# Memory projection and compression as float32 products, gates in one piece: a change to a two-layer decoder kernel

## The chip, the cores and the metric

The kernel runs on one core of one Trainium2 chip. The metric is the device time of one execution in microseconds (us); the median of several runs counts. Engines are named as the profile names them: PE is TensorE (PEld its weight loads), DVE is VectorE, ACT is ScalarE, POOL is GpSimd, SP is SyncE, which here only issues DMAs.

## What is computed

A decoder trunk of two layers on 512 tokens of width 1024, all in float32. Layer 0 is the one that the change touches. Its attention runs in three branches whose results are mixed by gates, beside a cross-attention to 256 memory tokens:

```python
mem_kv = rmsnorm(mem, mem_norm[layer]) @ w_mem_kv[layer]          # 256 x 1024 @ 1024 x 512
q, kc, vc, ks, vs, kw, vw, q_mem, gl = jnp.split(h @ a_w_in[i], A_SPLITS, axis=-1)

def compress(t, i):                                               # 31 blocks of 32 tokens, 3 heads
    tb = (t[:, :, blk_tok] + cmp_pos[i]).reshape(B, G, n_cmp, CMP_BLOCK * D)
    return jax.nn.gelu(tb @ cmp_w1[i] + cmp_b1[i]) @ cmp_w2[i] + cmp_b2[i]

gates = jax.nn.sigmoid(gate_logits)                               # 512 x 12 heads x 3 branches
return g_b[..., 0:1] * o_c + g_b[..., 1:2] * o_s + g_b[..., 2:3] * o_w
```

After attention come an output projection and a squared-ReLU MLP; layer 1 has dilated attention, the same memory attention with its own projection, and another MLP.

## The kernel before

**Products.** Nearly every large product is made of three products of type fp32r: an operand is split into a part rounded to fp32r and a residue, and `mm3` (L250 to L255) adds up high x high, high x residue and residue x high in PSUM. The split costs ScalarE a copy and VectorE or GpSimd a subtraction: `wsplit` (L246, L248) for weights, `part` (L269, L270) for activations with a gain, `split` (L288, L291) for the rest. Weights are fetched in tiles of 512 KB into a ring of three staging tiles `st` by SP's queue (`wload`, L234), and the split writes them to a ring of four working tiles `w`. A few products are plain float32: the probabilities times values (`pair`, L696, with two products side by side in the two halves of the array) and the last product of the compressed branch (L967).

**Order of the work.** The program is written as generators. In layer 0 a list of attention items (scores, softmax, scaling, transposes, output) runs in the foreground, and a list of background work is stepped at fixed ratios between the items. Within a generator, each `yield` is a place at which something else may come between. A scheduler then orders the instructions of each engine. Engines and DMA queues take their instructions strictly in that order.

**Start of layer 0.** `proj_a(0, ...)` makes queries, keys and values of the first head group; woven with its second half is the projection to `w_a0`, 420 columns wide (compressed keys and values, and 36 gate logits). Its evacuation `evac0` (L743 to L750) runs once for each of four blocks of 128 rows: ScalarE scales all 420 columns into a tile (L744), and the last 36 go through minus and clip (L747), exponential (L748), plus one (L749) and reciprocal (L750) to the sigmoid gates in the tile `ab`.

**The stage that the change touches.** Two generators are woven. `compress` makes for keys and for values: transposes of the projection (L805), copies of it and of a shifted copy (L811, L812), then in four steps sums with the position term on GpSimd (L825), a split (L288, L291), and 16 products of 96 x 256 (each one `mm3`) with the weights `w_c1`; `finish` applies the GELU (L844 to L853), transposes (L858) and multiplies by the small `w_c2` (six matmuls of 64 columns). `mem_kv(0, ...)` splits the normalised memory (L269, L270, 256 columns each) and makes 8 x 2 products of 128 x 512 (each one `mm3`) with `w_mem`, then the key norm and the values. Together they are the first entry of the background work; the projections of the next head groups follow.

**Softmax of the branches.** `attn_a`'s `front` makes the scores (L1004, L1017), the maximum (L1008, L1020) and the exponentials with their sums (L216), a reciprocal of the two sums (L1028), a multiplication of it by the two gates (L1029, 128 x 2), and GpSimd scales both probability tiles by that column (`pscale`, L684: two multiplications, the second by 1.0). `back` transposes the tiles (L1047, L1053).

## Time and profile before

| what | us |
|---|---|
| median of 3 runs | 1303.48 |
| lowest and highest of them | 1299.24 and 1312.04 |
| the profiled execution, its own time | 1296.79 |
| its span, from first to last instruction | 1295.0 |
| start of the 420-wide projection to the first product of the compression | 28.6 to 73.2 |
| compression and memory projection on TensorE | 73.2 to 107.2 |
| rest of the attention of layer 0 | 107.2 to 340 |

A row of the profile's views names the line, the engine, the operation and the tiles as output<-input, the shape, and how often; after the bar stand the busy time in us, the mean in ns, and the idle time just before, with what ended it. A row of a timeline begins with start and length in us. A row of windows begins with the stretch and its length, then gives by engine the busy time and the number of instructions (in the order PE, PEld, DVE, ACT, POOL), then the granted TensorE clock, the DMA share and GB/s; a window made for one line shows only the engines that run that line. A row of waits names who waited for whom, the total in us, how often, and the longest. A busy TensorE is not one at its peak, since the ends of its matmuls are modelled and overlap.

### The profile page before, as it was taken

How to read it: one execution, taken by the hardware profiler on the slowest of the kernel's cores; microseconds unless marked ns; L12 is line 12 of the kernel's file. 1: busy time of each engine (PE TensorE's matmuls, PEld its weight loads, DVE VectorE, ACT ScalarE, POOL GpSimd, SP SyncE). 2: the span in 40 equal slices, each digit the busy share in tenths (PEclk: the TensorE clock that was granted, in tenths of full speed). 3: DMA queues.
4: the chain of work that ended last, by engine and by line, in shares of the span. 5: the costliest groups of instructions: out<-in, count | busy, mean ns of one | idle time of the engine just before them, and what ended most of it. 6: DMA issues, size and time to landing. Idle time of an engine off the chain costs nothing.

```text
span 1295.0 us, 18552 instructions
## 1 busy us (share of the span) xinstructions
PE 1239.9 (96%) x6468; PEld 1026.0 (79%) x6468; DVE 858.9 (66%) x1597; ACT 770.5 (59%) x1699; POOL 380.9 (29%) x478
## 2 busy tenths in 40 slices
PE   9789998899999999999999989999999999999998
PEld 7668776678788888888887889887678888888887
DVE  6987767755565657566578567776667656656566
ACT  6775677774575364453657548777657445355462
POOL 4365684533140000000002779572424000000000
PEclk9899999999999999999999999999999999999999
DMA  7342322334478797897965331210249789698434
GB/s 262 116 128 89 98 98 90 66 75 115 139 248 232 239 267 221 261 234 222 284 202 176 104 112 50 69 45 9 85 151 291 217 271 245 211 282 231 141 111 162
DMA packets 61837, 215.28 MB, mean 166 GB/s; under 512 B 6736, under 2 KB 14928, under 8 KB 61232
## 3 DMA queue, kind: packets, MB, share of 16 engines
q1 hardware_dynamic: 50800, 143.72, 34.2%
q0 software_dynamic: 9344, 35.77, 14.0%
q10 hardware_dynamic: 1600, 34.61, 7.4%
q8 instruction: 51, 0.84, 0.3%
q14 instruction: 42, 0.34, 0.1%
HBM read 208.83 MB, written 72.35 MB: 217 GB/s over the span
## 4 chain that ended last, share of the span: by engine, by line
PE 67%; DVE 5%; ACT 4%; DMA 2%; POOL 2%; issue 2%; SPq 0%; POOLq 0%; ACTq 0%; DVEq 0%
PE s_ps L253 13%; PE s_ps L254 13%; PE s_ps L255 13%; PE s_acc L254 3%; PE s_acc L255 3%; PE s_acc L253 3%; PE s_pt L254 3%; PE s_pt L255 3%; PE s_pt L253 3%; PE s_po L696 2%; DVE s_w L248 1%; ACT s_p L216 1%; PE s_ps L1508 1%; ACT s_w L246 1%; DVE s_pt L216 1%
## 5 line engine op out<-in xcount | busy, mean ns | idle before, releaser
L248 DVE TENSOR_TENSOR s_w<-s_st,s_w 128x1024 fp32r<-128x1024 f32 (+3 forms) x240 | 287.1, 1200 | 256.7 <-ACT s_w L246 255.5
L246 ACT ACTIVATE s_w<-s_st 128x1024 fp32r<-128x1024 f32 (+4 forms) x272 | 263.8, 973 | 186.2 <-PE s_pt L255 44.0
L253 PE MATMUL s_ps<-s_act,s_w 128*128 128x512 f32 x568 | 221.7, 392 | 0.7 <-ACT s_act L288 0.7
L255 PE MATMUL s_ps<-s_act,s_w 128*128 128x512 f32 x568 | 221.8, 391 | 0.0
L254 PE MATMUL s_ps<-s_act,s_w 128*128 128x512 f32 x568 | 221.3, 390 | 0.0
L253 PEld LDWEIGHTS s_ps<-s_act,s_w 128*128 128x128 f32 x568 | 106.5, 188 | 23.8 <-ACT s_act L288 1.6
L255 PEld LDWEIGHTS s_ps<-s_act,s_w 128*128 128x128 f32 x568 | 106.6, 188 | 22.8 <-issue 0.8
L254 PEld LDWEIGHTS s_ps<-s_act,s_w 128*128 128x128 f32 x568 | 106.6, 188 | 21.9 <-DVE s_act L291 0.2
L216 ACT ACTIVATE s_p<-s_ps 128x512 f32<-128x512 f32 x64 | 38.2, 597 | 112.6 <-PE s_ps L255 112.6
L254 PE MATMUL s_acc<-s_w,s_act 128*128 128x512 f32 (+3 forms) x288 | 101.6, 354 | 3.1 <-POOL s_w L248 1.7
L253 PE MATMUL s_acc<-s_w,s_act 128*128 128x512 f32 (+3 forms) x288 | 101.3, 357 | 2.7 <-DVE s_tq L912 1.1
L1136 POOL DMA_DIRECT2D sum<-in_w_db_dram x16 | 14.4, 901 | 301.7 <-ACT s_p L216 300.0
L255 PE MATMUL s_acc<-s_w,s_act 128*128 128x512 f32 (+3 forms) x288 | 99.8, 351 | 0.0
L684 POOL TENSOR_SCALAR s_p<-s_p,s_cr 128x256 f32<-128x256 f32 (+3 forms) x128 | 73.5, 597 | 66.9 <-DVE s_cr L1029 14.5
L216 ACT ACTIVATE s_p<-s_ps,s_nm 128x256 f32<-128x256 f32 (+3 forms) x128 | 65.5, 522 | 16.3 <-DVE s_nm L1008 7.0
L248 POOL TENSOR_TENSOR s_w<-s_st,s_w 128x512 fp32r<-128x512 f32 (+4 forms) x32 | 55.4, 1732 | 50.0 <-ACT s_w L246 41.4
L253 PEld LDWEIGHTS s_acc<-s_w,s_act 128*128 128x128 f32 x288 | 54.5, 190 | 9.6 <-DVE s_tq L912 1.2
L254 PEld LDWEIGHTS s_acc<-s_w,s_act 128*128 128x128 f32 x288 | 54.7, 190 | 8.3 <-POOL s_w L248 2.3
L692 ACT ACTIVATE s_pt<-s_pt 128x512 f32<-128x512 f32 (+2 forms) x97 | 51.0, 529 | 15.5 <-PE s_pt L1053 5.4
L288 ACT ACTIVATE s_qk<-s_p 128x256 fp32r<-128x256 f32 (+1 forms) x96 | 46.9, 489 | 21.3 <-DVE s_p L1146 19.4
L255 PEld LDWEIGHTS s_acc<-s_w,s_act 128*128 128x128 f32 x288 | 54.6, 190 | 4.0
L1136 POOL DMA_DIRECT2D sum<-sum x16 | 14.1, 883 | 146.1 <-DMA sum<-sum 50.3
(334 smaller groups left out, 2959.2 us busy)
## 6 DMA issues: line engine op xcount, KB each, us to landing
s_st<-in_w_up_dram SPq DMA_DIRECT2D x64, 512.0 KB, 4.2
s_st<-sum SPq DMA_DIRECT2D x64, 512.0 KB, 6.8
s_st<-in_w_db_dram SPq DMA_DIRECT2D x48, 512.0 KB, 4.5
sum<-in_w_db_dram POOLq DMA_DIRECT2D x16, 1024.0 KB, 13.9
sum<-sum POOLq DMA_DIRECT2D x16, 1024.0 KB, 10.6
s_st<-in_w_bq_dram SPq DMA_DIRECT2D x16, 384.0 KB, 3.3
s_st<-in_w_ag_dram SPq DMA_DIRECT2D x11, 512.0 KB, 4.7
s_st<-in_w_c_dram SPq DMA_DIRECT2D x8, 512.0 KB, 3.6
```

What stands on the lines that cost most here:

```text
L216: return lambda *a, **k: self.marks.append(f(*a, **k))
L246: nc.scalar.activation(w[:, 0], st, AF.Copy)
L248: e.tensor_tensor(out=w[:, 1], in0=st, in1=w[:, 0], op=ALU.subtract)
L253: mm(ps, lh[0], rh[0], start=start, stop=False, skip_group_check=again)
L254: mm(ps, lh[0], rh[1], start=False, stop=False, skip_group_check=again)
L255: mm(ps, lh[1], rh[0], start=False, stop=stop, skip_group_check=again)
L288: nc.scalar.activation(dst[:, 0], src, AF.Copy)
L684: self.nc.gpsimd.tensor_scalar(out=p, in0=p, scalar1=c, scalar2=1.0, op0=ALU.mult, op1=ALU.mult)
L692: self.turned = self.nc.scalar.activation(dst, src, AF.Copy)
L696: i = self.nc.tensor.matmul(*a, **k)
L1136: self.behind(self.nc.gpsimd.dma_start(t[o], x, accum_op=ALU.add, max_dma_last_dim=4096))
L1508: nc.tensor.matmul(Sp[:, o + g * P : o + g * P + P], q4[1 + g][:, s, blk], kp4[hl][:, s, blk], start=ii == 0 and g == 0 and hl == 0, stop= ...
```

## The change

Three things are changed, and everything behind layer 0's attention stays as it is.

1. The first layer's memory projection is a generator of its own, `mem_kv_whole`: the memory is scaled by ScalarE alone into a float32 tile, the weights are fetched by two DMAs into one working tile (`wpair`) without staging and without a split, and each product is one float32 product. Layer 1's projection keeps the three fp32r products.
2. The compression does likewise: its sums with the position term are used as they are, `w_c1` comes through `wpair`, and the products with `w_c1` and `w_c2` are float32.
3. `evac0` writes only the scaled logits for each block; after the fourth block one chain of four instructions on 144 columns makes all gates. The multiplication of reciprocal and gates (L1029) is gone: `pscale` takes the gate's column as its second multiplier in place of 1.0.

The core of the diff (evaluation of the key norm, `mem_out`, is the old code moved):

```diff
+    def wpair(self, src, i):
+        w = self.t("w", [P, 2, src.shape[-1]])
+        for j in range(2):
+            self.nc.sync.dma_start(w[:, j], src[i + j])
+        return w
...
+    def mem_kv_whole(self, l, res):
...
+            st = self.t("st", [P, 4, NMEM])
+            nc.sync.dma_start(st, ins["memT"][j])
+            a = self.t("act", [P, 4, NMEM])
+            for i in range(4):
+                k = j * 4 + i
+                nc.scalar.activation(a[:, i, :], st[:, i, :], AF.Copy, scale=g[:, k : k + 1])
...
+        for k in range(KT):
+            if k % 4 == 0:
+                w = self.wpair(ins["w_mem"][l], k // 2)
+            for b in range(2):
+                nc.tensor.matmul(
+                    banks[b], tiles[k // 4][:, k % 4, b * P : (b + 1) * P],
+                    w[:, k % 4 // 2, k % 2 * 512 : k % 2 * 512 + 512], start=k == 0, stop=k == KT - 1,
+                )
+            yield
...
-    def pscale(self, p, c):
-        self.nc.gpsimd.tensor_scalar(out=p, in0=p, scalar1=c, scalar2=1.0, op0=ALU.mult, op1=ALU.mult)
+    def pscale(self, p, c, g=1.0):
+        self.nc.gpsimd.tensor_scalar(out=p, in0=p, scalar1=c, scalar2=g, op0=ALU.mult, op1=ALU.mult)
...
-            t = self.t("x", [P, 420])
-            nc.scalar.activation(t, ps, AF.Copy, scale=st[0][:, b : b + 1])
+            t = self.t("x", [P, 384])
+            nc.scalar.activation(t, ps[:, 0:384], AF.Copy, scale=st[0][:, b : b + 1])
             raw0.append(t)
-            ga = gt[:, b, :]
-            nc.vector.tensor_scalar(out=ga, in0=t[:, 384:420], scalar1=-1.0, scalar2=80.0, op0=ALU.mult, op1=ALU.min)
+            nc.scalar.activation(gt[:, b, :], ps[:, 384:420], AF.Copy, scale=st[0][:, b : b + 1])
+            if b < NB - 1:
+                return
+            ga = ab[:, 0:144]
+            nc.vector.tensor_scalar(out=ga, in0=ga, scalar1=-1.0, scalar2=80.0, op0=ALU.mult, op1=ALU.min)
             nc.scalar.activation(ga, ga, AF.Exp)
...
-        work.add(weave(comp, chain(self.mem_kv(0, kf)), RC[2]), "cmp")
+        work.add(weave(comp, self.mem_kv_whole(0, kf), RC[2]), "cmp")
...
-            ws = []
             for j in range(4):
-                while len(ws) < min(4, j + 2):
-                    ws.append(self.wload(ins["w_c1"][which, len(ws)]))
+                if j % 2 == 0:
+                    w = self.wpair(ins["w_c1"][which], j)
...
-                tb = self.t("qki", [P, 2, 4, 96], F32R)
-                self.split(tb, tbf.rearrange("p i g c -> p i (g c)"))
                 for i in range(4):
-                    self.mm3(
-                        ps, [tb[:, h, i, :] for h in (0, 1)],
-                        [ws[j][:, h, i * 256 : (i + 1) * 256] for h in (0, 1)],
-                        j == 0 and i == 0, j == 3 and i == 3,
+                    nc.tensor.matmul(
+                        ps, tbf[:, i].rearrange("p g c -> p (g c)"), w[:, j % 2, i * 256 : (i + 1) * 256],
+                        start=j == 0 and i == 0, stop=j == 3 and i == 3,
                     )
...
             nc.vector.reciprocal(out=c, in_=sm)
-            nc.vector.tensor_tensor(out=c, in0=c, in1=gt[:, i, o : o + 2], op=ALU.mult)
             for br in range(2):
-                self.pscale(p[br], c[:, br : br + 1])
+                self.pscale(p[br], c[:, br : br + 1], gt[:, i, o + br : o + br + 1])
```

The scheduler moves instructions as well. On VectorE, in the stretch behind the 420-wide projection, this stood between two of the casts that write the first group's keys (s_qk_124; the casts are L665 before and L703 after; s_ab_117 are the gates, s_w_738 and s_w_743 weights of the compression):

```order
L665 CAST s_qk_124<-s_pt_440 128x2x128
L747 TENSOR_SCALAR s_ab_117<-s_x_625 128x36
L708 TENSOR_TENSOR s_tq_520<-s_tq_520,s_r_98_517 128x384
L749 TENSOR_SCALAR s_ab_117<-s_ab_117 128x36
L750 RECIPROCAL s_ab_117<-s_ab_117 128x36
L248 TENSOR_TENSOR s_w_738<-s_st_736,s_w_738 128x1024
L660 TENSOR_TENSOR s_qki_529<-s_tq_520,s_qki_529 128x6x64
L248 TENSOR_TENSOR s_w_743<-s_st_741,s_w_743 128x1024
L665 CAST s_qk_124<-s_pt_502 128x2x128
```

and now stands:

```order
L703 CAST s_qk_124<-s_pt_440 128x2x128
L746 TENSOR_TENSOR s_tq_517<-s_tq_517,s_r_98_514 128x384
L514 SCALAR_TENSOR_TENSOR s_r_109_570<-s_r_107_564,ec_303,s_r_108_566 128x6
L698 TENSOR_TENSOR s_qki_526<-s_tq_517,s_qki_526 128x6x64
L703 CAST s_qk_124<-s_pt_499 128x2x128
```

Of the nine rows the three gate operations and the two subtractions are gone from between the casts. On GpSimd, at the first scalings (L684 before, L722 after) and the sums of the compression (L825 before, L865 after; s_tmp are the sums of its four steps, s_ab the gates), the last sums stood before all scalings of 384 columns:

```order
L825 TENSOR_TENSOR s_tmp_879<-s_x_678,c_115 128x4x31
L825 TENSOR_TENSOR s_tmp_746<-s_x_679,c_115 128x4x31
L825 TENSOR_TENSOR s_tmp_790<-s_x_679,c_115 128x4x31
L825 TENSOR_TENSOR s_tmp_847<-s_x_679,c_115 128x4x31
L825 TENSOR_TENSOR s_tmp_879<-s_x_679,c_115 128x4x31
L684 TENSOR_SCALAR s_p_205_1029<-s_p_205_1029,s_cr_1033 128x384
L684 TENSOR_SCALAR s_p_206_1030<-s_p_206_1030,s_cr_1033 128x384
```

and now one of those scalings stands ahead of them:

```order
L865 TENSOR_TENSOR s_tmp_787<-s_x_669,c_115 128x4x31
L722 TENSOR_SCALAR s_p_182_884<-s_p_182_884,s_cr_888,s_ab_117 128x384
L865 TENSOR_TENSOR s_tmp_719<-s_x_670,c_115 128x4x31
L865 TENSOR_TENSOR s_tmp_740<-s_x_670,c_115 128x4x31
L865 TENSOR_TENSOR s_tmp_770<-s_x_670,c_115 128x4x31
L865 TENSOR_TENSOR s_tmp_787<-s_x_670,c_115 128x4x31
L722 TENSOR_SCALAR s_p_183_885<-s_p_183_885,s_cr_888,s_ab_117 128x384
```

So the first compression product has one more scaling ahead of it on GpSimd, and every scaling now reads the gates. On TensorE the memory projection and the first compression stay interleaved, with fewer and longer products, and on SP's queue three of the next group's weight fetches now stand ahead of the compression's, which wait for TensorE to release a working tile.

More of the change, by code (lines that the diff above doesn't have):

```diff
@@ L538, in mem_stats, with mem_out, mem_kv @@
         return self.meancols(ss)
-    def mem_kv(self, l, res, banks=None):
+    def mem_kv_whole(self, l, res):
+        nc, ins = self.nc, self.ins
+        g = self.gcol(f"mem{l}")
+        tiles, ws = [], []
+        for j in range(2):
+            st = self.t("st", [P, 4, NMEM])
[4 more added lines that the diff above has]
+                nc.scalar.activation(a[:, i, :], st[:, i, :], AF.Copy, scale=g[:, k : k + 1])
+            tiles.append(a)
+        yield
+        banks = [self.ps(self.pacc, [P, 512]) for _ in range(2)]
+        for k in range(KT):
[6 more added lines that the diff above has]
+                )
+            yield
+        t = self.t("act", [P, 2, 2, 256])
+        kf = [[t[:, b, w, :] for w in range(2)] for b in range(2)]
+        for b in range(2):
+            self.mem_out(kf[b], banks[b], b)
+            yield
+        res.append(kf)
+    def mem_out(self, kf, ps, b):
+        nc = self.nc
+        r, e = self.ms
+        nc.scalar.activation(kf[1], ps[:, 256:512], AF.Copy, scale=r[:, b : b + 1])
+        f = self.normf(ps[:, 0:256], 4, e[:, b])
+        nc.vector.tensor_tensor(
+            out=kf[0].rearrange("p (h d) -> p h d", d=HD),
+            in0=ps[:, 0:256].rearrange("p (h d) -> p h d", d=HD), in1=bcast(f, 2, HD), op=ALU.mult,
+        )
+    def mem_kv(self, l, res):
         nc, ins = self.nc, self.ins
@@ L552, in mem_kv @@
                 tiles.append(a)
[L553 removed]
         yield
[L556 to L568 removed]
+        kf = [[self.t("tmp", [P, 256]) for _ in range(2)] for _ in range(2)]
+        def evac(b, ps):
+            self.mem_out(kf[b], ps, b)
         stat = lambda k, b: [tiles[k // 2][:, h, k % 2, b * P : (b + 1) * P] for h in (0, 1)]
[L571 removed]
+        yield from self.proj(None, ins["w_mem"][l], 512, evac, blocks=2, stat=stat, lo="gv", banks=[self.pacc] * 2)
         res.append(kf)
@@ L869, in finish @@
                 for kt in range(2):
-                    self.mm3(ps, [gT[:, h, kt, :] for h in (0, 1)], [w2[:, h, kt, :] for h in (0, 1)], kt == 0, kt == 1)
+                    nc.tensor.matmul(ps, gT[:, kt, :], w2[:, kt, :], start=kt == 0, stop=kt == 1)
                 kr = self.t("tmp", [96, HD])
@@ L890, in finish @@
                 for kt in range(2):
-                    self.mm3(ps, [gT[:, h, kt, :] for h in (0, 1)], [w2[:, h, kt, :] for h in (0, 1)], kt == 0, kt == 1)
+                    nc.tensor.matmul(ps, gT[:, kt, :], w2[:, kt, :], start=kt == 0, stop=kt == 1)
                 nc.vector.tensor_tensor(out=vc, in0=ps, in1=b2, op=ALU.add)
```

23 lines of the change are left out of this document (4 added, 19 removed).

## The prediction

> **What bounds the kernel now.** I read the page first, then the windows by stage, then the waits of TensorE and the timelines of VectorE and GpSimd in the stages that the change touches. Line numbers are those of the kernel before, unless said otherwise.
>
> ```profile
> span 1295.0 us, 18552 instructions
> PE 1239.9 (96%) x6468; PEld 1026.0 (79%) x6468; DVE 858.9 (66%) x1597; ACT 770.5 (59%) x1699; POOL 380.9 (29%) x478
> ```
>
> TensorE is busy for 96% of the span. What it saves or gains in work shows in the end, and so do the 55 us in which it stands still. The program's windows say where those are (us, then busy time by engine):
>
> ```profile
> 33.60:52.50 18.90, 16.45 (x92) 15.36 (x90) 18.90 (x52) 11.69 (x38) 8.55 (x8) 1.00 0.26 85
> 52.50:73.10 20.60, 13.06 (x67) 9.78 (x66) 19.63 (x42) 18.16 (x51) 12.05 (x25) 0.83 0.32 102
> 73.10:107.20 34.10, 30.39 (x194) 25.77 (x195) 29.14 (x55) 23.84 (x49) 19.27 (x31) 1.00 0.50 153
> 107.20:340.00 232.80, 215.06 (x1356) 169.92 (x1355) 149.27 (x400) 149.86 (x447) 118.50 (x171) 1.00 0.32 90
> ```
>
> The change lies in the first three. From 33.6 to 73.1 VectorE (third number) is busy in 38.5 of 39.5 us, TensorE in 29.5: here VectorE is the bound, and TensorE loses 10.0 us, plus a granted clock of 0.83 over the second stretch. From 73.1 to 107.2 (memory projection, compression) TensorE misses 3.7 us. The waits of TensorE between 30 and 107 us name the releaser:
>
> ```profile
> PE s_ps L1004 <- DVE s_qk L665: 5.2, 1, 5.2
> PE s_pt L717 <- DVE s_qki L660: 2.3, 1, 2.3
> PE s_pt L253 <- DVE s_r L507: 1.3, 1, 1.3
> PE s_po L696 <- DVE s_pt L690: 1.2, 1, 1.2
> PE s_acc L254 <- DVE s_w L248: 1.1, 2, 0.8
> ```
>
> All five end with VectorE, 11.1 us together. What VectorE does ahead of the longest one (start, length):
>
> ```profile
> 52.92 0.38 DVE L750 RECIPROCAL s_ab<-s_ab 128x36 f32<-128x36 f32 x1
> 53.22 1.38 DVE L248 TENSOR_TENSOR s_w<-s_st,s_w 128x1024 fp32r<-128x1024 f32 x1
> 54.52 0.94 DVE L660 TENSOR_TENSOR s_qki<-s_tq,s_qki 128x384 fp32r<-128x384 f32 x1
> 55.39 1.84 DVE L248 TENSOR_TENSOR s_w<-s_st,s_w 128x1024 fp32r<-128x1024 f32 x1
> 57.16 0.41 DVE L665 CAST s_qk<-s_pt 128x256 fp32r<-128x256 f32 x1
> ```
>
> A gate operation and two residue subtractions of compression weights (L248), none needed until 73 us, stand in line ahead of the keys (L665) that TensorE waits for.
>
> **What the change takes from VectorE.** The groups of VectorE between 33.6 and 73.1 us that go or shrink, and the weights' group (windows of L248) from 73.1 to 107.2:
>
> ```profile
> L248 DVE TENSOR_TENSOR s_w<-s_st,s_w 128x1024 fp32r<-128x1024 f32 x4 | 5.6, 1412 | 0.0
> L270 DVE SCALAR_TENSOR_TENSOR s_act<-s_st,gv,s_act 128x256 fp32r<-128x256 f32 x8 | 5.3, 707 | 0.0
> L1029 DVE TENSOR_TENSOR s_cr<-s_cr,s_ab 128x2 f32<-128x2 f32 x6 | 2.0, 354 | 0.0
> L747 DVE TENSOR_SCALAR s_ab<-s_x 128x36 f32<-128x36 f32 x4 | 2.0, 494 | 0.0
> L749 DVE TENSOR_SCALAR s_ab<-s_ab 128x36 f32<-128x36 f32 x4 | 1.5, 374 | 0.0
> L750 DVE RECIPROCAL s_ab<-s_ab 128x36 f32<-128x36 f32 x4 | 1.5, 366 | 0.0
> L1028 DVE RECIPROCAL s_cr<-s_su 128x2 f32<-128x2 f32 x6 | 0.9, 156 | 0.0
> 73.10:107.20 34.10, 13.35 (x11) 0.00 (x0) 1.00 0.50 153
> ```
>
> Ahead of 73.1: the four L248, the eight L270 and the six L1029 go whole (12.9 us). The twelve gate operations (5.0 us) become three of 144 columns. A reciprocal of 2 columns takes 0.156 us and one of 36 takes 0.366, so 6.2 ns a column and about 1.0 us for 144; with two cheap ones some 1.5 us. VectorE loses about 16.4 of 38.5 us there. After 73.1 eight of the eleven L248 belong to the changed weights, 9.7 us.
>
> **First term: the start of the compression, -8.5 us.** VectorE will no longer set this stage; what is late next must be found. I follow the chain from TensorE's last product of the 420-wide projection to its first of the compression:
>
> ```profile
> 51.30 0.36 PE L255 MATMUL s_ps<-s_w,s_act 128*128 128x420 f32 x1
> 73.16 0.36 PE L253 MATMUL s_acc<-s_w,s_qki 128*96 128x256 f32 x1
> ```
>
> The projection ends at 51.6, with the 2.3 us wait inside it: about 49.3 without. The change puts all four gates into one chain behind the last evacuation: ScalarE copy, VectorE, two exponentials of the first scores and the gates' own on ScalarE, VectorE again with the 1.0 us reciprocal. My estimate for it is 5.7 us: the 1.5 us of gate operations from above, and 4.2 for four evacuations and exponentials of about 0.6 with the hops between engines. So the gates stand at about 55. Before, only block 0's gate was needed for the first scaling; now all are. From there GpSimd sets the pace, as before:
>
> ```profile
> 64.38 0.73 POOL L684 TENSOR_SCALAR s_p<-s_p,s_cr 128x128 f32<-128x128 f32 x2 [8.22 <-DVE s_cr L1028]
> 65.28 2.54 POOL L684 TENSOR_SCALAR s_p<-s_p,s_cr 128x256 f32<-128x256 f32 x6 [0.17 <-DVE s_cr L1029]
> 67.78 5.01 POOL L825 TENSOR_TENSOR s_tmp<-s_x,c 128x124 f32<-128x124 f32 x12
> ```
>
> First scaling to last addition took 8.4 us. The order now puts one 128x384 scaling ahead of the last four additions, so some 9.0, and another 0.6 to the matmul: 55 + 9.6 = 64.6 against 73.16, a gain of 8.5. ScalarE covers this: it loses four L246 in the stretch. The bounds: not more than TensorE's idle 10.0 us plus the lost clock (0.17 of 13.1 us busy, 2.2), so -12.2; not less than -2, should only the 2.3 us wait go and the gates' chain come late.
>
> **Second term: float32 products on TensorE, +7.6 us.** The memory projection issues 16 products in place of 48, of 512 columns; the compression 32 in place of 96, of 256 columns; the last step 4 in place of 12, of 64 columns (nothing). First the pitch of the fp32r products (two rows that follow each other, of 256 columns; a window of the MLP, all 512 columns), then the two kinds of float32 product of 512 columns in the trace; each product is recorded as two matmuls:
>
> ```profile
> 75.21 0.28 PE L255 MATMUL s_acc<-s_w,s_qki 128*96 128x256 f32 x1
> 75.33 0.28 PE L253 MATMUL s_acc<-s_w,s_qki 128*96 128x256 f32 x1
> 500.00:600.00 100.00, 100.00 (x443) 82.81 (x442) 63.35 (x87) 48.00 (x65) 3.52 (x4) 1.00 0.81 240
> 312.51 1.13 PE L967 MATMUL s_po<-s_x,s_vcb 128*128 128x512 f32 x2
> 313.48 0.60 PE L638 MATMUL s_pt<-c,s_p 128*128 128x128 f32 x4
> 323.51 1.94 PE L696 MATMUL s_po<-s_pt,s_act 128*64 128x512 f32 x8
> 325.38 0.50 PE L254 MATMUL s_acc<-s_act,s_w 128*128 128x512 f32 x1
> ```
>
> An fp32r product costs 100 / 443 = 0.226 us (512) or 0.12 us (256) from start to start. A float32 one of 512 costs 0.97 (312.51 to 313.48). The four half-array products L696 run two at a time and take 1.87, 0.935 a pair. I take 0.935, and half of it for 256 columns. Memory: 16 x 0.935 - 48 x 0.226 = +4.1. Compression: 32 x 0.468 - 96 x 0.12 = +3.5. Together +7.6. [...] The columns stream from 73 to 107 us, where TensorE is all but full, so nothing hides them.
>
> [...]
>
> **Third term: waits inside the projection, -2.5 us.** The last three waits above (3.6 us) lie behind VectorE, which loses 9.7 us of weights and, with L291, the splits of activations of its 29.1:
>
> ```profile
> 73.10:107.20 34.10, 5.79 (x10) 1.00 0.50 153
> ```
> I count 2.5 of 3.6, since the shorter chains still have their own latency. Bounds -3.6 and +1: weights now land straight in the working buffers, whose transfers wait in SP's queue for TensorE to release a buffer, with attention's weights queued behind. Before, they landed in staging tiles. The last compression pair waits for the memory product of row block 1; I see some 5 us of margin. On GpSimd the bias transfer now waits for a compression product, with the next scalings behind it; by the order those come 10 us later than TensorE needs anything else, so zero.
>
> **Fourth term: the small multiplication, -1 us.** 48 L1029 go, and L684 multiplies by a column in place of 1.0; it had two multiplications already. From 107 to 345 us:
>
> ```profile
> POOL s_p L684 <- DVE s_cr L1029: 14.3, 10, 3.2
> PE s_pt L1053 <- POOL s_p L684: 1.2, 2, 1.0
> ```
>
> GpSimd waits long for L1029, but TensorE waits for the scaled tile only 1.2 us. So -1, with 0 and -3 as bounds. A second column on GpSimd is not in this trace; no price to +3 us, were the 96 scalings to slow enough to reach those waits. I take none, as both multiplications exist.
>
> **The sum.** -8.5 + 7.6 - 2.5 - 1.0 = -4.4 us. The profiled execution took 1296.8 us (span 1295.0 and 1.8 around it); it becomes 1292.4. It lies 6.7 us below the median of the three runs shown, 1303.5, so I forecast 1299 as the median. The best corner is -12.2 + 4.7 - 3.6 - 3 = -14.1, the worst -2 + 8.7 + 1 + 3 = +10.7.
>
> **Rivals.** *The gates' chain holds the start back (slower).* All four gates must exist before the first scaling; if that comes at 62 rather than 55, the start gains 2 us, and TensorE's dearer products decide: -2 + 7.6 - 1 - 0.5 = +4.1, so 1307.5. It decides from a first scaling later than about 59.5, where the sum is zero. For it speaks that GpSimd stood idle for 8.2 us on VectorE's L1028; against it, that VectorE loses 16 us just ahead.
>
> *Attention gains too.* From 107 to 340 us TensorE misses 17.7 us; without 48 small operations, and with buffers free sooner, half could go: -4.4 - 8.8 = -13.2, so 1290. Against it: most of those waits are for ScalarE's exponentials, which stay.
>
> *Cheap float32 products.* L967 and L696 stand alone in their stages; in a long run of float32 products each recorded pass might go at the fp32r pitch. Then a product costs 2 x 0.226 or 2 x 0.12, the second term is 16 x 0.452 - 10.8 + 32 x 0.24 - 11.5 = -7.4, the sum -19.4, the time 1284. Against it: L967's two passes start 0.5 apart with nothing else at hand. [...]
>
> *Late weights.* The buffer waits in SP's queue add 5 us to the forecast: 1304.
>
> **Chances.** Forecast 0.50, gates' chain 0.20, attention gains 0.16, cheap products 0.05, late weights 0.09. Faster by over 1% (below 1290.4; 1% is about what a measurement of this kernel can tell from no change) holds half of attention, the cheap products and a little of the forecast: 0.17. Slower by over 1% (above 1316.5) needs the worst corner and more: 0.05. The rest is 0.78. The range, 1286 to 1311, takes the best corner, 1289, with 3 us for runs nearer to the profiled one, and the worst corner less its last 3 us.
>
> **What would show it.** Right: the first compression matmul near 64 to 65 us, GpSimd's first scaling near 55, float32 products of 512 columns about 0.94 us apart with no idle between them, VectorE 35 to 40 us less busy in all, TensorE's products in memory and compression 7 to 8 us longer, and after 107 us the same picture shifted by 4 to 6. Wrong: a first scaling after 60, a clock below 1 during the float32 products, waits of TensorE for DMA in the compression, or scalings of 128x128 that take longer than 0.37 us.

## The result, and the profile after

The changed kernel takes 1296.5 us in the median of 10 runs (1293.8 to 1302.8), beside 1303.7 for the kernel before, in 10 runs too: ratio 0.9946, 95% interval 0.9927 to 0.9965. A second measurement (below) gives 0.9948 (0.9930 to 0.9967). So it is 7 us faster, by 0.5%. But the profiled executions lie much closer, 1296.1 and 1296.8 us, and that is the riddle of this case.

The page of the changed kernel (span; busy time, share and instructions of each engine):

```profile
span 1294.3 us, 18328 instructions
PE 1244.8 (96%) x6416; PEld 1021.6 (79%) x6416; DVE 825.1 (64%) x1502; ACT 756.5 (58%) x1684; POOL 379.0 (29%) x478
```

VectorE has lost 33.8 us, TensorE has gained 4.9. The same four stretches as in the prediction, then all the rest:

```profile
33.60:52.50 18.90, 17.31 (x98) 16.50 (x98) 15.83 (x41) 13.62 (x44) 10.97 (x11) 1.00 0.49 160
52.50:73.10 20.60, 18.10 (x81) 11.49 (x82) 12.58 (x29) 15.27 (x48) 12.28 (x25) 1.00 0.38 151
73.10:107.20 34.10, 33.63 (x154) 23.36 (x152) 16.40 (x35) 13.75 (x35) 12.13 (x27) 1.00 0.40 131
107.20:340.00 232.80, 215.96 (x1352) 170.79 (x1352) 142.00 (x357) 151.06 (x448) 125.51 (x171) 0.99 0.31 85
340.00:1294.30 954.30, 927.94 (x4595) 774.88 (x4593) 615.61 (x1001) 541.04 (x1072) 204.62 (x227) 1.00 0.62 185
```

From 33.6 to 73.1 VectorE (third number) is busy for 28.4 in place of 38.5 us, TensorE for 35.4 in place of 29.5, and the clock of the second stretch is 1.00 in place of 0.83. From 73.1 to 107.2 TensorE stands still for 0.5 us in place of 3.7. Its longest waits from 30 to 107 us, in place of 5.2 and 2.3:

```profile
PE s_pt L765 <- ACT s_qk L705: 1.0, 2, 0.9
PE s_pt L755 <- DVE s_qki L698: 1.0, 1, 1.0
PE s_acc L260 <- DVE s_tq L947: 0.8, 1, 0.8
```

The chain of the first term, on VectorE (the gates' last steps), GpSimd and TensorE:

```profile
55.33 0.22 DVE L790 TENSOR_SCALAR s_ab<-s_ab 128x144 f32<-128x144 f32 x1
55.58 1.05 DVE L791 RECIPROCAL s_ab<-s_ab 128x144 f32<-128x144 f32 x1
```

```profile
56.84 0.88 POOL L722 TENSOR_SCALAR s_p<-s_p,s_cr,s_ab 128x128 f32<-128x128 f32 x2 [5.16 <-ACT s_qk L761]
58.35 3.04 POOL L722 TENSOR_SCALAR s_p<-s_p,s_cr,s_ab 128x256 f32<-128x256 f32 x6 [0.63 <-DVE s_cr L1063]
```

```profile
66.23 1.03 PE L867 MATMUL s_acc<-s_w,s_tmp 128*96 128x256 f32 x4
73.11 5.34 PE L867 MATMUL s_acc<-s_w,s_tmp 128*96 128x256 f32 x24
78.29 1.88 PE L566 MATMUL s_acc<-s_w,s_act 128*128 128x512 f32 x4
80.52 7.08 PE L566 MATMUL s_acc<-s_w,s_act 128*128 128x512 f32 x16
87.44 0.33 PE L895 MATMUL s_pt<-c,s_raw 96*128 96x96 f32 x2
```

The gates are ready at 56.6 and the first scaling follows 0.2 us later (the profile puts its wait down to a ScalarE copy; the gates came last). The first compression product starts at 66.23 in place of 73.16. Each product is again recorded as two matmuls: 12 of 256 columns take 78.29 - 73.11 = 5.18 us, 0.432 each; 8 of 512 take 87.44 - 80.52 = 6.92, 0.865 each, with no idle between them.

### The profile page after: what moved, and what is told of

Same layout as the page of the kernel before. It is cut to its first block, busy times and chain, and to the rows that moved or that the text cites. A ratio compares the mean times of both kernels' runs of the same rounds, so it can differ in the third digit from the quotient of the medians.

```text
span 1294.3 us, 18328 instructions
## 1 busy us (share of the span) xinstructions
PE 1244.8 (96%) x6416; PEld 1021.6 (79%) x6416; DVE 825.1 (64%) x1502; ACT 756.5 (58%) x1684; POOL 379.0 (29%) x478
## 4 chain that ended last, share of the span: by engine, by line
PE 80%; DVE 8%; ACT 6%; POOL 3%; issue 2%; DMA 2%; POOLq 0%; ACTq 0%; DVEq 0%
PE s_ps L261 14%; PE s_ps L262 13%; PE s_ps L260 13%; PE s_acc L260 5%; PE s_acc L261 5%; PE s_acc L262 5%; PE s_po L734 3%; PE s_pt L261 3%; PE s_pt L262 3%; PE s_pt L260 3%; DVE s_w L255 2%; ACT s_p L216 1%; PE s_ps L1542 1%; PE s_acc L867 1%; PE s_acc L566 1%
## 5 line engine op out<-in xcount | busy, mean ns | idle before, releaser
L255 DVE TENSOR_TENSOR s_w<-s_st,s_w 128x1024 fp32r<-128x1024 f32 (+3 forms) x228 | 272.0, 1197 | 254.7 <-ACT s_w L253 253.7
L253 ACT ACTIVATE s_w<-s_st 128x1024 fp32r<-128x1024 f32 (+4 forms) x260 | 251.3, 970 | 186.8 <-PE s_pt L262 41.1
L260 PE MATMUL s_ps<-s_act,s_w 128*128 128x512 f32 x568 | 222.1, 393 | 1.4 <-ACT s_act L295 1.4
L260 PEld LDWEIGHTS s_ps<-s_act,s_w 128*128 128x128 f32 x568 | 106.5, 188 | 25.2 <-ACT s_act L295 3.2
L260 PE MATMUL s_acc<-s_w,s_act 128*128 128x512 f32 (+3 forms) x272 | 94.9, 354 | 3.6 <-DVE s_tq L947 2.2
L261 PE MATMUL s_acc<-s_w,s_act 128*128 128x512 f32 (+3 forms) x272 | 95.1, 351 | 2.0 <-POOL s_w L255 1.8
L262 PE MATMUL s_acc<-s_w,s_act 128*128 128x512 f32 (+3 forms) x272 | 93.7, 350 | 0.0
L722 POOL TENSOR_SCALAR s_p<-s_p,s_cr,s_ab 128x128 f32<-128x128 f32 (+3 forms) x96 | 60.3, 664 | 47.9 <-DVE s_cr L1063 26.4
L255 POOL TENSOR_TENSOR s_w<-s_st,s_w 128x512 fp32r<-128x512 f32 (+4 forms) x32 | 54.6, 1706 | 63.6 <-ACT s_w L253 63.5
L216 ACT ACTIVATE s_p<-s_ps,s_nm 128x256 f32<-128x256 f32 (+3 forms) x128 | 65.5, 523 | 9.6 <-DVE s_nm L1043 2.8
L260 PEld LDWEIGHTS s_acc<-s_w,s_act 128*128 128x128 f32 x272 | 51.7, 191 | 9.7 <-DVE s_tq L947 1.5
L261 PEld LDWEIGHTS s_acc<-s_w,s_act 128*128 128x128 f32 x272 | 51.9, 191 | 6.3 <-POOL s_w L255 2.4
L262 PEld LDWEIGHTS s_acc<-s_w,s_act 128*128 128x128 f32 x272 | 51.9, 191 | 3.6
```

Of the source, the lines that this page charges most:

```text
L216: return lambda *a, **k: self.marks.append(f(*a, **k))
L253: nc.scalar.activation(w[:, 0], st, AF.Copy)
L255: e.tensor_tensor(out=w[:, 1], in0=st, in1=w[:, 0], op=ALU.subtract)
L260: mm(ps, lh[0], rh[0], start=start, stop=False, skip_group_check=again)
L261: mm(ps, lh[0], rh[1], start=False, stop=False, skip_group_check=again)
L262: mm(ps, lh[1], rh[0], start=False, stop=stop, skip_group_check=again)
```

## The experiments

Every run is timed against the kernel before on its own chip (medians 1301.1, 1303.2 and 1302.4 us for the three groups of four). "At 678" is how much later than in the profile of before the transposes at the end of layer 0's MLP begin (677.87 us there), "layer 1" the time from there to the end of the span, with the number of steps of 3.41 us at half clock in it (explained below). First scaling, first compression product, 678 and layer 1 are read from one profiled execution of each kernel.

| run | median us, ratio to before (interval) | first scaling | first compression product | at 678 | layer 1 |
|---|---|---|---|---|---|
| before | | 64.4 | 73.2 | 0 | 617.1 (2) |
| changed | 1296.5, 0.9946 (0.9927-0.9965) | 56.8 | 66.2 | -5.9 | 622.4 (2) |
| gates and scaling alone | 1310.2, 1.0065 (1.004-1.009) | 64.7 | 74.7 | +5.7 | 624.5 (4) |
| both float32 parts alone | 1300.8, 0.9997 (0.998-1.0013) | 55.8 | 68.7 | -0.8 | 623.7 (5) |
| memory projection alone | 1299.0, 0.9984 (0.9965-1.0003) | 60.4 | 69.7 | -0.1 | 617.3 (3) |
| compression alone | 1307.9, 1.0051 (1.003-1.0071) | 62.1 | 73.8 | +4.7 | 626.4 (8) |
| gates' chain alone | 1307.2, 1.0037 (1.0008-1.0065) | 65.7 | 76.0 | +8.4 | 616.3 (3) |
| changed, VectorE copies weights | 1301.5, 0.9992 (0.9969-1.0015) | 67.0 | 73.0 | -0.2 | 620.4 (3) |
| changed, memory products twice | 1311.9, 1.0063 (1.0036-1.009) | 56.6 | 65.9 | +9.3 | 625.3 (5) |
| before, 13 warm-up products | 1315.7, 1.0087 (1.0052-1.0123) | 64.8 | 78.3 | +10.1 | 619.2 (2) |
| changed, again | 1295.8, 0.9948 (0.993-0.9967) | 56.5 | 65.9 | -6.9 | 623.1 (4) |
| changed, gates by block | 1296.1, 0.9944 (0.9921-0.9967) | 55.8 | 66.4 | -7.7 | 620.1 (3) |
| changed, multiplication kept | 1297.1, 0.9954 (0.9935-0.9972) | 58.0 | 66.4 | -4.6 | 619.4 (2) |
| changed, layer 1's memory too | 1292.8, 0.9925 (0.9896-0.9954) | 56.1 | 65.5 | -9.0 | 621.6 (3) |

### The parts by themselves

Each takes the kernel before and one part of the change's diff. The first, gates and scaling:

```diff
+            if b < NB - 1:
+                return
+            ga = ab[:, 0:144]
...
-            nc.vector.tensor_tensor(out=c, in0=c, in1=gt[:, i, o : o + 2], op=ALU.mult)
+                self.pscale(p[br], c[:, br : br + 1], gt[:, i, o + br : o + br + 1])
```

> The kernel before with the third change alone: gates in one chain after the fourth block, and no small multiplication of reciprocal and gates; the products stay fp32r with their splits. Theory V (the gain is VectorE's work ahead of the compression): of VectorE's 38.5 busy us between 33.6 and 73.1 this takes only some 5.5 (nine small gate operations and six small multiplications), and the two subtractions of 1.4 and 1.8 us stay ahead of the keys, so the first compression matmul comes at 70 to 72 in place of 73.2 and the whole gains 1 to 3 us: about 1301.5. Rival G (the gates and the 48 small multiplications bring the gain, the float32 products only pay for themselves): 5 to 7 us faster, about 1297.5, most of it gained after 107 us.

Both theories were wrong: it is 9 us slower. The place is on GpSimd, whose first scaling waits for the gates:

```profile
64.67 2.82 POOL L684 TENSOR_SCALAR s_p<-s_p,s_cr,s_ab 128x128 f32<-128x128 f32 x6 [7.71 <-DVE s_ab L753]
```

The chain that ends at 56.6 in the changed kernel ends 8 us later here, at 64.5, since VectorE still makes the subtractions of weights ahead of its steps and between them (the next section shows such rows). This is the prediction's slower rival, in a kernel that has only this part.

Both float32 parts, then each alone (the diff's `mem_kv_whole` and the diff's `compress`):

```diff
-        work.add(weave(comp, chain(self.mem_kv(0, kf)), RC[2]), "cmp")
+        work.add(weave(comp, self.mem_kv_whole(0, kf), RC[2]), "cmp")
```

```diff
-                self.split(tb, tbf.rearrange("p i g c -> p i (g c)"))
...
+                    nc.tensor.matmul(
+                        ps, tbf[:, i].rearrange("p g c -> p (g c)"), w[:, j % 2, i * 256 : (i + 1) * 256],
```

> The kernel before with both float32 changes (memory projection and compression) and the gates and the small multiplication as before. Theory V: VectorE loses 5.6 (four subtractions of weights) and 5.3 us (eight of activations) ahead of 73 us, so the first compression matmul comes at 67 to 69; the products cost TensorE 5.3 us more (16 of 0.865 and 32 of 0.432 in place of 48 of 0.226 and 96 of 0.12), and the waits inside 73 to 107 (3.6 us) go: -5 + 5.3 - 3.5, about 1300.5. Rival G: the products pay only for themselves, 1303 to 1304.

> The kernel before with the memory projection alone as float32 products; compression, gates and small multiplication as before. Theory V: VectorE loses the eight subtractions of activations (5.3 us) ahead of 73 but keeps the two subtractions of compression weights ahead of the keys: first compression matmul at 70 to 72; the 16 products cost +3.0 us (0.865 each); part of the 3.6 us of waits goes: about 0 in all, 1302 to 1305. Rival G gives the same time, 1303 to 1305, with no earlier start.

> The kernel before with the compression alone as float32 products (its weights fetched without staging and split); memory projection, gates and small multiplication as before. Theory V: the two subtractions ahead of the keys go, so the 5.2 us wait of TensorE for the keys shrinks to 1 to 2 us and the first compression matmul comes at 68 to 70; the 32 products cost +2.3 us (0.432 each): about 1300.5. Rival G: no gain, 1303 to 1306.

Together they start the compression at 68.7, as theory V had it, and reach the first scores of the compressed branch 2.9 us ahead of before, near theory V's 3.2. At 678 only 0.8 are left, with two half-clock steps at 194 us that before does not have, and the time is level with before, as rival G had it: 1300.8 lies near theory V's figure only because before takes 1301.1 on this chip. The memory projection alone starts earlier than either theory had it (69.7) and takes 2.1 us less than before, with an interval that reaches no change.

The compression alone goes against both theories. The wait for the keys shrinks to 1.4 us, as theory V had it, but its start comes no earlier (73.8), so that its dearer products are not paid for. One cause lies in an operation that the changed kernel no longer makes, the small multiplication of reciprocal and gates. The same stands in the run with both float32 parts (GpSimd, VectorE, then TensorE's last row ahead of the first compression product):

```profile
61.68 5.01 POOL L862 TENSOR_TENSOR s_tmp<-s_x,c 128x124 f32<-128x124 f32 x12
63.34 3.37 DVE L1061 TENSOR_TENSOR s_cr<-s_cr,s_ab 128x2 f32<-128x2 f32 x1
68.17 0.69 PE L1079 MATMUL s_pt<-c,s_p 128*128 128x128 f32 x2 [2.34 <-ACT s_x L850]
```

The multiplication of two columns (the next one, at 68.60, takes 0.14 us) takes 3.37 us and ends with GpSimd's twelve sums; behind it stand a copy on VectorE, one on ScalarE, and TensorE's wait of 2.34 us. With the compression alone it takes 3.38 us and the wait is 2.36. Against the changed kernel's 66.2 the start at 68.7 is 2.4 us late, about this wait. So the third part, which loses by itself, removes what holds up the other two. Either half of it is enough: the runs below with gates by block and with the multiplication kept both start at 66.4.

Set against before, the three parts alone make +9, -2 and +7 us, and the whole makes -7. They do not add up.

### Gates' chain without the scaling, and an edit that changes only the order

```diff
+            ga = ab[:, 0:144]
...
             nc.vector.tensor_tensor(out=c, in0=c, in1=gt[:, i, o : o + 2], op=ALU.mult)
```

> The kernel before with the gates in one chain after the fourth block, but with the small multiplication of reciprocal and gates kept; all products fp32r. Layer 1's attention keeps the instruction order of before (in the run with gates and scaling together it had the order of the changed kernel). Theory H (with VectorE still full, one chain for all gates holds the first scaling back): the first scaling comes at 64 to 66 and waits for the gates, the first compression matmul at 73 to 76, and the event times behind 120 us lie 3 to 5 us after those of before; in all 3 to 5 us slower, 1304 to 1306. Rival O (the loss of the run with gates and scaling together came from layer 1's order alone): no loss up to 690 us, 1300 to 1302.

The rows of VectorE show the subtraction (L248) between two steps of the chain (L750, L752) and the end of the chain:

```profile
58.31 0.22 DVE L750 TENSOR_SCALAR s_ab<-s_ab 128x144 f32<-128x144 f32 x1
60.64 1.21 DVE L248 TENSOR_TENSOR s_w<-s_st,s_w 128x1024 fp32r<-128x1024 f32 x1
61.84 0.21 DVE L752 TENSOR_SCALAR s_ab<-s_ab 128x144 f32<-128x144 f32 x1
62.91 1.04 DVE L753 RECIPROCAL s_ab<-s_ab 128x144 f32<-128x144 f32 x1
```

Theory H held for the first scaling (65.7), the start (76.0) and the median (4 us slower), but at 678 the run lies 8.4 us behind, not 3 to 5. Then the kernel before with two more of the small products at its start:

```diff
-NW = 11
+NW = 13
```

> The kernel before with 13 in place of 11 of the small products at the very start, which run while TensorE waits for its first data; nothing else is edited. The scheduler answers with another order in layer 0's first 110 us and puts the last part of layer 1's attention, some 140 TensorE instructions between about 885 and 947 us, in exactly the order of the changed kernel. Theory O (this order costs 4 to 5 us): the event times of this stretch drift by +4 to +5 us against before, 1304 to 1307 in all if layer 0 stays level. Rival P (the order costs nothing; what the changed kernel lost there is the phase of the half-clock stretches): drift of 0 to 2 us, 1300 to 1302.

It is 12 us slower than before, the slowest of all, although beyond these two products it computes nothing new: the scheduler puts TensorE's instructions in another order. The waits of TensorE from 45 to 120 us, and the windows from 33.6 to 120 us of before and of this run, show what that does:

```profile
PE s_ps L1017 <- ACT s_p L216: 3.3, 2, 3.0
PE s_pt L717 <- ACT s_qk L723: 2.9, 1, 2.9
PE s_pt L717 <- DVE s_qki L660: 2.7, 1, 2.7
PE s_acc L253 <- ACT s_qki L288: 1.8, 1, 1.8
```

```profile
33.60:120.00 86.40, 72.71 (x421) 61.91 (x420) 78.14 (x174) 59.04 (x152) 43.97 (x67) 0.96 0.39 120
```

```profile
33.60:120.00 86.40, 68.65 (x371) 57.50 (x372) 71.37 (x153) 55.44 (x140) 40.40 (x63) 0.92 0.36 115
```

The 5.2 us wait for the keys is gone, but before has only 0.5 of the first of these waits, 2.3 of the third and none of the others. TensorE is idle for 4.1 us more in these 86 us, and its clock is 0.04 lower, by an estimate another 3.5 (0.04 of 86.4). So this run's order is worse than that of before by some 7.5 us in this stage. Order is one reason why the parts do not add up, beside the multiplication that took 3.37 us and the gates' chain, which costs where VectorE is full (here) and not where it has room (the run with gates by block, below); what of each part's loss is order and what is its work, these runs do not separate further.

Layer 1 shows the same. Its code is untouched, but by the order the last part of its attention (some 140 TensorE instructions) stands in the changed kernel as in the run with gates and scaling, the run with 13 products and the last one of the table, while the memory projection alone and the chain alone keep nearly the order of before. Layer 1 takes 616.3 to 617.3 us in the three profiles with before's order, and 619.2 to 624.5 in the five with the changed kernel's: means 616.9 and 622.2. With 1.7 us taken off for each half-clock step (half of its 3.41 us, an estimate), 612.4 and 617.1. The stretch itself shows it more clearly. From a transpose at 907.05 us of before (L717) to a product at 949.12 (L255) it takes 42.1 us in before and 41.5 and 42.3 in the two others with its order; the same work takes 46.6 in the changed kernel, 47.3 in its second profile, 46.1 with gates and scaling, 46.5 with 13 products and 46.6 in the last run of the table. So some 4.5 us of what the change gains go there, as theory O had it: in the changed kernel TensorE stands still for 4.5 us of it in place of 2.0, and a half-clock step falls into it. (The whole of layer 1 hides this in the run with 13 products, 619.2 in place of 617.1, because that run lacks a half-clock step that before has at 693.65.)

### Is it VectorE's relief?

```diff
-            self.nc.sync.dma_start(w[:, j], src[i + j])
+            st = self.wdma(src[i + j])
+            self.nc.vector.tensor_tensor(out=w[:, j], in0=st, in1=st, op=ALU.max)
```

> The changed kernel, but the twelve weight tiles of 128x1024 of memory projection and compression are fetched into the staging tiles again and VectorE writes each to the working tile with a two-input operation (the larger of the tile and itself), in place of the subtraction that it made before; products, gates and scaling as in the changed kernel. Theory V (the gain up to 340 us is VectorE's relief): VectorE has 12 x 1.4 = 17 us back, some 5.6 ahead of 73 us; the first compression matmul comes at 69 to 73 in place of 66.2, and the events at 340 us 3 to 6 us later than in the changed kernel: 1299 to 1302. Rival D (the relief of VectorE does not matter; what counts is gates and scaling): first compression matmul at 66 to 67, within 1 us of the changed kernel, 1295 to 1296.5.

VectorE, GpSimd and TensorE of this run:

```profile
53.18 1.51 DVE L249 TENSOR_TENSOR s_w<-s_st 128x1024 f32<-128x1024 f32 x1
55.08 1.21 DVE L249 TENSOR_TENSOR s_w<-s_st 128x1024 f32<-128x1024 f32 x1
61.04 0.23 DVE L791 TENSOR_SCALAR s_ab<-s_ab 128x144 f32<-128x144 f32 x1
64.57 1.03 DVE L792 RECIPROCAL s_ab<-s_ab 128x144 f32<-128x144 f32 x1
```

```profile
66.98 3.87 POOL L723 TENSOR_SCALAR s_p<-s_p,s_cr,s_ab 128x128 f32<-128x128 f32 x8
```

```profile
72.97 1.10 PE L868 MATMUL s_acc<-s_w,s_tmp 128*96 128x256 f32 x4
```

With the weights back on VectorE the gates are ready at 65.6 in place of 56.6, the compression starts at 73.0, and of the 5.9 us gained at 678 only 0.2 are left. The start and the time are as theory V forecast, but the load is heavier than it reckoned: eight of the twelve copies, 10.7 us, run ahead of 73.1, where the kernel before has four subtractions, 5.6 us. In all VectorE is busy for 36.9 us from 33.6 to 73.1, beside 38.5 in before and 28.4 in the changed kernel. GpSimd's order has changed too: four of the compression's sums stand ahead of the first scaling. So with the same float32 products the gain goes when VectorE is filled again; how much of that is load and how much is order, the run does not separate.

### The price of a float32 product

```diff
-            for b in range(2):
+            for b in (0, 1, 0, 1):
                 nc.tensor.matmul(
                     banks[b], tiles[k // 4][:, k % 4, b * P : (b + 1) * P],
...
```

> The changed kernel with each of the sixteen 512-column float32 products of the memory projection issued twice in a row into the same sum (memory keys and values are therefore twice as large before the key norm). TensorE is full in this stage, so the extra products show their price. Theory M (0.865 us each, as the changed kernel's rows have it): +13.8 us against the changed kernel. The prediction's price (0.935): +15.0. Cheap products (0.452): +7.2. With the changed kernel some 6 us under before, that is about 1309, 1310 or 1302.

TensorE's longest piece of these products, and what follows it:

```profile
87.11 12.23 PE L567 MATMUL s_acc<-s_w,s_act 128*128 128x512 f32 x28
99.18 1.03 PE L869 MATMUL s_acc<-s_w,s_tmp 128*96 128x256 f32 x4
```

14 products take 12.07 us, 0.862 each, the price in theory M. In the whole time the 16 products cost 1.5 us more than that (8.7 above before where the changed kernel is 6.6 below it on another chip: 15.3); the time alone would fit the prediction's price as well, the row does not.

### The small parts within the changed kernel, and one step further

The changed kernel, unedited:

> The changed kernel once more, unedited, as the yardstick on this chip. Theory: about 7 us under before (1295 to 1297), with a first profile's picture: no wait of TensorE over 1.5 us between 30 and 110 us, no half-clock stretch there, first compression matmul at 66. If the gain of the two medians were the chance of one chip, the interval would reach zero here.

It repeats its gain. Then with the gates by block again:

```diff
-            if b < NB - 1:
-                return
-            ga = ab[:, 0:144]
...
+            ga = gt[:, b, :]
```

> The changed kernel with the gates made for each of the four blocks again (twelve small VectorE operations in place of three), float32 products and the gates inside the scaling as in the changed kernel. GpSimd's order stays the same, TensorE's differs in some 20 rows near 50 us and in the last part of layer 1's attention (another order than before's and the changed kernel's). Theory H (the one chain holds the first scaling back, at 56.8 rather than 55): first scaling at 54 to 56, events at 340 us 0 to 2 us earlier. Theory V (VectorE's time ahead of the keys decides): VectorE has 3.5 us back, first scaling at 57 to 60, events at 340 us 0 to 3 us later. Layer 1's other order may add -3 to +1 behind 885 us. In all 1293 to 1299.

The first scaling comes at 55.8, as theory H had it, and the median lies within 0.3 us of the changed kernel's: once VectorE has room, the single chain neither gains nor costs anything that this measurement can tell. Then with the multiplication kept:

```diff
+            nc.vector.tensor_tensor(out=c, in0=c, in1=gt[:, i, o : o + 2], op=ALU.mult)
-                self.pscale(p[br], c[:, br : br + 1], gt[:, i, o + br : o + br + 1])
+                self.pscale(p[br], c[:, br : br + 1])
```

> The changed kernel with the 48 small multiplications of reciprocal and gates back on VectorE and the scaling by one column and 1.0; products and the single gates' chain as in the changed kernel. The prediction's term for this part is 1 us (0 to 3): events at 340 us 0 to 3 us later than in the changed kernel, 128x128 scalings at 0.37 in place of 0.44 us. Theory O (what such an edit does to the order of instructions outweighs its work, as in the two runs of before that lost 4 and 12 us by it): a shift of 4 us or more by 125 us, of either sign.

It costs 1.3 us in the median, little beside the 6 us and more over which each kernel's runs spread; theory O failed here, the order does not fall apart. The run also shows what the second column costs GpSimd: the same scalings from 30 to 345 us, with the constant (this run, first) and with the gates' column (changed kernel).

```profile
L722 POOL TENSOR_SCALAR s_p<-s_p,s_cr 128x384 f32<-128x384 f32 x24 | 13.9, 594 | 14.9 <-DVE s_cr L1064 9.2 <-ACT s_p L216 2.6 <-ACT s_qki L697 1.8
L722 POOL TENSOR_SCALAR s_p<-s_p,s_cr 128x128 f32<-128x128 f32 x24 | 10.0, 439 | 7.2 <-DVE s_cr L1064 6.2 <-DVE s_cs L978 0.2 <-PE s_pt L1088 0.2
```

```profile
L722 POOL TENSOR_SCALAR s_p<-s_p,s_cr,s_ab 128x384 f32<-128x384 f32 x24 | 16.4, 705 | 18.6 <-DVE s_cr L1063 16.1 <-PE s_pt L1087 2.4
L722 POOL TENSOR_SCALAR s_p<-s_p,s_cr,s_ab 128x128 f32<-128x128 f32 x24 | 11.4, 515 | 7.1 <-ACT s_qk L761 5.2 <-DVE s_cr L1063 1.2 <-DVE s_c L984 0.7
```

By these means a scaling takes 0.08 to 0.11 us longer with the column. The means hold some long ones too (the kernel before, with the constant, has 0.498 and 0.615); the middle one of the 24 takes 0.372 with the constant (0.376 in before) and 0.452 with the column at 128x128, 0.585 (0.590) and 0.665 at 128x384: about 0.075 us at both widths. It is hidden: from 107 to 340 us TensorE waits 0.2 us for scaled tiles, 1.2 in before. Last, layer 1's memory projection as float32 products too:

```diff
...
-        work.add(self.mem_kv(1, self.kf1))
+        work.add(self.mem_kv_whole(1, self.kf1))
```

> The changed kernel with layer 1's memory projection (which runs in the background of layer 0's attention, near 200 us) as sixteen float32 products too, without its splits of weights and activations; TensorE's order is the same up to that place and again in layer 1's attention. Theory T (float32 products pay only where VectorE is the bound; here TensorE is busy for 88 to 93 per cent and most of its waits are for ScalarE's exponentials): +3 us by the products (16 of 0.865 in place of 48 of 0.226), up to 1 us of it given back: 1298 to 1300 where the changed kernel has 1296.5. Rival F (relief of VectorE and ScalarE pays here as well): -2 to -5 us, 1291 to 1295.

This went against my theory T: 1292.8, the fastest kernel of the study, 9.6 us under before and 3.0 under the changed kernel on the same chip (six runs; the 3.0 are only just clear of the spread). From 107 to 340 us these waits of TensorE shrink or go (changed kernel first):

```profile
PE s_po L734 <- ACT s_pt L730: 2.6, 5, 1.2
PE s_acc L260 <- DVE s_tq L947: 1.4, 1, 1.4
```

```profile
PE s_po L737 <- ACT s_pt L733: 0.9, 4, 0.3
```

```profile
107.20:340.00 232.80, 219.65 (x1344) 168.04 (x1344) 137.04 (x347) 149.08 (x448) 118.63 (x169) 1.00 0.32 89
```

TensorE is busy for 219.7 in place of 216.0 us, of which 3.0 are the dearer products; it stands still for 3.7 us less, and a half-clock stretch at 173 us is gone. So it may be that even where VectorE is busy for only 60 per cent, splits stand ahead of something that TensorE waits for. Whether it is the relief itself or the order that came with it, this one run doesn't tell.

## Why the prediction was right in its mechanism and near in its number by two errors

**Start of the compression, -8.5.** Measured -6.9 (73.16 to 66.23), by the named mechanism: the run with the copies undoes it. The gates came at 56.6, not 55. The chain took 5.3 us, near the 5.7 estimated, and from the gates to the first product it took 9.6, as forecast; what was wrong is where the chain begins. The 420-wide projection ends at 51.3 in the changed kernel, not at 49.3: of the 2.3 us wait inside it 1.0 stayed (L755), and another of 0.8 came (L260). One reading of the start was off as well: the gates of each block are needed by scalings from 64.4 on, not only from 73.

**Float32 products, +7.6.** Mis-sized: +5.3. A product of 512 columns costs 0.86 in this run of products, not the 0.935 of L696, which I took because it was nearest in form: 16 x 0.865 - 10.8 = +3.0 and 32 x 0.432 - 11.5 = +2.3. The +4.7 that the best corner has for this term is shown by no run; the runs showed +5.3. The +8.7 of the worst corner is the term with 0.97 for a product, the row of L967. By the rows a float32 product costs 3.8 times an fp32r one at 512 columns (0.865 against 0.226) and 3.6 times at 256 (0.432 against 0.12).

**Waits from 73 to 107, -2.5.** Too small. From the first compression product to the first scores of the compressed branch (113.66 before, 107.01 after) it takes 40.5 us before and 40.8 after: +0.3, so with +5.3 for the products some 5.0 went. TensorE's idle time gives 3.2 of it. Two of the next projection's products fall outside this stretch in the changed kernel, another 0.5; the rest I can't place.

**The multiplication, -1.** The size fits: its return costs 1.3 us. What I had not seen is that beside GpSimd's sums it can take 3.4 us and delay the start of the compression, as in the two runs above; in the run that only puts it back into the changed kernel the longest one near the start takes 0.97 us and the start does not move (66.4). The second column's price, which I had set to nothing, is about 0.075 us a scaling on GpSimd, and hidden. So the scalings of 128x128 did come out longer than 0.37 us, one of my signs of being wrong, without costing time.

At the first scores the gain is 6.65 us, at 678 it is 5.9 (6.9 in the second profile), where the sum said 4.4.

**"After 107 us the same picture shifted."** This failed. It holds up to the end of layer 0; then the other order in layer 1's attention takes about 4.5 us back, and the profiled execution comes out 0.7 us faster, not 4.4.

**The 6.7 us from the profiled execution to the median.** This failed too, in the other direction. I carried the distance over as if it were a constant. The changed kernel's median lies 0.4 us above its profiled execution. The distance goes with the time at half clock, and the change takes some of that away. Before, in the stretches of 3.41 us around the long wait (the clock stands behind the engines' numbers):

```profile
48.53:51.94 3.41, 3.41 (x23) 3.31 (x22) 3.41 (x12) 1.25 (x5) 1.40 (x2) 1.00 0.00 0
51.94:55.36 3.42, 0.61 (x6) 0.40 (x4) 3.38 (x5) 3.42 (x5) 3.26 (x4) 1.00 0.00 0
55.36:58.77 3.41, 1.06 (x4) 0.99 (x5) 3.41 (x5) 2.38 (x7) 0.79 (x1) 0.50 0.69 185
58.77:62.18 3.41, 3.34 (x17) 2.72 (x17) 2.78 (x7) 3.18 (x11) 0.00 (x0) 0.50 0.74 257
```

The changed kernel, in the same stretches (its own grid of such steps, explained below, lies half a step off; there no step from 43 to 80 us holds more than 0.9 us of idle):

```profile
51.94:55.36 3.42, 2.37 (x16) 1.64 (x15) 2.41 (x8) 3.33 (x13) 0.00 (x0) 1.00 0.93 367
55.36:58.77 3.41, 2.65 (x14) 1.71 (x14) 3.20 (x8) 3.37 (x15) 1.30 (x3) 1.00 1.02 416
58.77:62.18 3.41, 2.65 (x15) 1.78 (x14) 2.48 (x7) 3.32 (x11) 3.41 (x8) 1.00 0.34 137
```

A stretch in which TensorE worked for 0.61 us is followed by one at half clock, that one (1.06) by another. In the changed kernel TensorE works for 2.4 us or more of each and keeps its clock. In the 14 profiles of this study, those in which the compression starts at 68 us or later have two to four half-clock steps between 53 and 81 us; those with a start before 67 have none or one. Over the 86 runs of before beside the experiments, mean clock and time go together (correlation -0.85): median 1296.3 us at a clock of 0.993 or more, 1306.3 at 0.9875 or less. Its median clock on the three chips is 0.990, 0.9885 and 0.990; the changed kernel's, in its two measurements, 0.9935 and 0.993. The profiled execution of before, with 0.995, was one of its best. So the 7 us of the medians are about -6 up to 678 us, +5 in layer 1, most of it by its order, and -6 that are left over. For these last the runs show only the correlation: the straight line through the 86 runs gives 3.4 us for a clock of 0.9935 in place of 0.990, and the rest stays open. The forecast of 1299 thus came near 1296.5 partly by luck: the 5 us that layer 1 took back and the 6 us by which the two distances differ were both missed, and they cancel.

**The rivals.** The gates' chain: the first scaling at 56.8 lies before the 59.5 from which it would decide; in the kernel before, without the other parts, it does decide, with a first scaling at 64.7 and 65.7. Attention: TensorE's busy time from 107 to 340 us is 216.0 against 215.1, so little was gained there. Cheap products: no, by the prices above (0.865 and 0.432, where that rival has 0.452 and 0.24). Late weights: TensorE waits for no transfer in this stage; it does so once, for 1.9 us, in the run with the memory projection alone.

## What to carry to other kernels

A float32 product in place of three fp32r products costs TensorE 20 to 28 per cent more here (0.432 against 3 x 0.12, 0.865 against 3 x 0.226) and frees the two engines that split; it paid here where those engines' work stood ahead of something that TensorE waits for (5.9 us gained at 678), and, as one run suggests, even where they are far from full (3.0 us, with VectorE busy for about 60 per cent). A part of a change that gains inside the whole can lose by itself, and where a scheduler sets the order, an edit with next to no work of its own (two small products) moved the time by 12 us: look at the order of every stage, also of those that the edit does not touch. The profiled execution may be a lucky one; compare its granted clock with that of the timed runs, and do not carry its distance to the median over to another kernel.

## What the runs showed of the hardware that was not expected

**Half clock after part of an idle stretch.** In the 14 profiles all half-clock stretches last 3.41 us or a multiple, and within one execution they begin on one grid of 3.41 us (before: 55.36, 693.65 and 758.50, apart by 187 and 19 steps), which lies otherwise in the next execution. They follow steps of the grid in which TensorE stood still for part of the time. In the changed kernel a step with 1.64 us of idle in its 3.41 is followed by one:

```profile
169.57:172.99 3.42, 1.78 (x13) 1.42 (x13) 3.39 (x10) 2.79 (x9) 3.09 (x5) 1.00 0.47 161
172.99:176.40 3.41, 3.41 (x19) 3.41 (x18) 3.00 (x10) 1.98 (x7) 3.05 (x5) 0.50 0.00 0
```

In the 14 profiles, from 30 us on, all 31 full-clock steps with 1.85 us of idle or more were followed by a step at half clock; so were 31 of the 186 with 1.0 to 1.85 us, and 6 of the 4875 with less. Between 1.0 and 1.85 us these traces do not say what decides. So by an estimate from these steps a wait of 2 us that lies within one of them costs its 2 us and up to 1.7 more (half of 3.41) where TensorE is the bound, and one that the grid cuts in two mostly only the 2 (155 of the 186 steps with 1.0 to 1.85 us of idle were followed by full clock). That may be why runs of one kernel differ by 10 us; it is not shown.

**A second column as multiplier** on GpSimd costs about 0.075 us an operation at the three widths measured: the middle one of 24 takes 0.452 against 0.376 us at 128x128, 0.665 against 0.590 at 128x384 and 0.772 against 0.697 at 128x512 (the changed kernel and before).

**A small VectorE operation beside GpSimd's sums.** A multiplication of 128x2, which can take 0.14 us, takes 3.37 and 3.38 us in two runs and 1.02 in before; each of the three ends within 0.03 us of the last of GpSimd's back-to-back sums. That it is held by them is read from these times; no run tests it.
